# Gate sums moved into the attention stage and onto Pool, output groups on two sets of PSUM banks, last outputs issued from two queues

## The chip, the core and the metric

One core of one Trainium2 chip runs the whole kernel in one launch. The metric is device time in microseconds (us); the kernel before took 942.1 us, the median of 3 runs. TensorE (PE) does the products, VectorE (DVE) and ScalarE (ACT) work around them, GpSimd (POOL) is mostly free, and SyncE (SP) issues the transfers in the order of its queue. Each engine works through its own queue in order: an instruction that waits holds up all that stand behind it on that engine.

## What is computed

A transformer layer over 512 tokens of width 2048, in fp32. The part that matters here is the modulation: one row `mod = silu(c) @ w_ada + b_ada` is cut into shift, scale and **gate**, 2048 values each. Shift and scale are needed at the very start, gate only at the very end.

```python
mod = silu(c) @ w_ada[l] + b_ada[l]
shift, scale, gate = jnp.split(mod, 3, axis=-1)
h = rms_norm(x, norm_g[l]) * (1.0 + scale) + shift
z = h @ w_in[l]                       # u_A v_A gate_A | q k v gate_B forget_B
y_a = chunked_spatial_gating(gelu(u_a), gelu(v_a), ...) * silu(g_a)   # group A
y_b = forgetting_attention(q_b, k_b, v_b, f_b, b_f[l]) * silu(g_b)    # group B, 16 heads
y = concat([y_a, y_b]) @ w_out[l]
x = x + gate * y
return rms_norm(x, final_g)
```

## The kernel before, in words

Every weight tile is loaded as fp32 into a buffer of the ring `raw` (4 buffers, 512 KB loads), split by `w_tile` (L115) into a high part `whi` on ACT (L127) and a low part `wlo` on DVE (L128), and used in three products (hi times hi, hi times low, low times hi), so that one weight tile is 24 products of 512 columns. `whi` and `wlo` have two buffers each, so a tile is split while the tile before it is multiplied.

The stages, in the order in which PE goes through them:

- to about 240 us: shift and scale, the normalised input, the columns of u_A and part of gate_A;
- to about 620 us: branch B in four rounds u = 0 to 3 of four heads each. `g_group`, `qk_group` and `v_group` (L646 to L689) stream four weight tiles each for the gate, q, k and v columns. After each weight tile `tick()` (L131) takes one piece of attention from `slots` (scores, `lse`, probabilities, values: L472) and one piece from `fillers`. `lse` sends a row of sums back into q by eight small transfers on SP (L511), for which the second product of the probabilities waits (L528). `evac_q` clears two rows of q on POOL (L458) once that product has read the q of the round before;
- to about 710 us: the columns of v_A (`va`, L699), then `ga`, the last 256 columns of gate_A, with the mixing over chunks of branch A (`mix_head`, L727, which takes its PSUM banks by the tag `x`);
- to the end: the output projection in four groups of 512 columns (L816 to L857). Each group accumulates in four PSUM banks with the tag `mm` (`wob`, L818), one for each block of 128 tokens, and `wo_evac` (L783) multiplies a bank by the gate (L793), which also frees the bank, adds x (L799) and sums squares. The last group works from weights that were split ahead (`load_w3`, L808), block by block, and each block ends in the final norm and four output transfers from SP (L857).

PSUM has eight banks: four with the tag `mm`, and four (tags `b` and `c`) which `bank("x", ...)` (L59) gives out in turn.

**Gate** is summed in 32 steps, `gate_step(g, i)` (L594): a step loads 512 KB of `w_ada` into a buffer of the same ring `raw`, by SP, and DVE multiplies it by the values of silu(c) and adds it to `gate[:, g]`: 16 rows of 128 x 512 for each of the four groups, the first by L601 and the others by L603. `gate_sum(g)` (L605) then adds over the partitions by a product with ones (L610) and adds the bias (L611). These 36 pieces are put into `fillers` after round u = 3 (L691), and the ticks of `va`, `ga` and the output groups 0 and 1 work them off.

The order of the instructions is not the order of the code: a scheduler places each engine's instructions, so the change moves them on every queue.

Of the kernel before, what the change touches and what calls it, by code (L numbers as in the profile page):

```python
# [12 lines left out]
ALU = mybir.AluOpType  # L13
AX = mybir.AxisListType

P = 128
# [3 lines left out]
NT = S // P  # L20
# [7 lines left out]
def trunk_kernel(  # L28
# [30 lines left out]
    def bank(tag, name):  # L59
        if tag == "x":  # L60
            tag = "bbbc"[turn[0] % 4]
            turn[0] += 1
        return ps.tile([P, 512], F32, tag=tag, name=name, bufs={"mm": 4, "b": 3, "c": 1}[tag])
# [2 lines left out]
        nc.scalar.activation(hi, src, AF.Copy)  # L66
        (eng or nc.vector).tensor_tensor(lo, src, hi.bitcast(F32), ALU.subtract)

# [1 line left out]
    ident = const.tile([P, P], F32, name="ident")  # L70
    make_identity(nc, ident)
    cmask = const.tile([P, S], BF16, name="cmask")
# [17 lines left out]
        nc.vector.tensor_scalar(dst, src, mult, EPS, ALU.mult, ALU.add)  # L90
        nc.gpsimd.tensor_tensor(dst, dst, nhalf[:, 0:1], ALU.pow)

# [1 line left out]
    queue = []  # L94
    CHAIN = [1]

# [68 lines left out]
            for b in range(nb):  # L165
                evs[b](banks[b])

# [1 line left out]
    st_cm = tc.tile_pool(name="st", bufs=1)  # L169
    st = st_cm.__enter__()  # L170

# [246 lines left out]
                            evac_g(b - 8, sp[b], st)  # L418
    st_cm.__exit__(None, None, None)

# [1 line left out]
    pb_cm = tc.tile_pool(name="pb", bufs=1)  # L422
    pb = pb_cm.__enter__()
    QS = [[pb.tile([P, S], F32R, tag="qstk", bufs=8, name=f"q{i}_{j}") for j in range(2)] for i in range(4)]
# [165 lines left out]
        nc.vector.tensor_tensor_scan(f3, f1, f4, 0.0, ALU.mult, ALU.add)  # L590
        split(fsplit[:, 0, :], fsplit[:, 1, :], f3)

    # gate part of the modulation, worked off between weight tiles
    def gate_step(g, i):  # L594
        ga = wp.tile([P, 2, 512], F32, tag="raw", name=f"gate{g}_{i}", bufs=4)
        nc.sync.dma_start(ga, ada_r[:, 2 * i : 2 * i + 2, 2, g * 512 : (g + 1) * 512])
        for j in range(2):
            kk = 2 * i + j
            a = gate[:, g, :]
            if kk == 0:  # L600
                nc.vector.tensor_scalar(a, ga[:, j], sc[:, 0:1], None, ALU.mult)  # L601
            else:
                nc.vector.scalar_tensor_tensor(a, ga[:, j], sc[:, kk : kk + 1], a, ALU.mult, ALU.add)  # L603

    def gate_sum(g):  # L605
        gsl = slice(2 * D + g * 512, 2 * D + (g + 1) * 512)
# [3 lines left out]
        nc.tensor.matmul(gp, ones, gate[:, g, :], start=True, stop=True)  # L610
        nc.vector.tensor_tensor(gate[:, g, :], gp, bg, ALU.add)  # L611

    # spatial weights, worked off between weight tiles
    bias2 = gp_.tile([P, 8, P], F32, name="bias2")

    def spatial_weights():
# [49 lines left out]
    def g_group(u):  # L666
        col_group([(GB0 + u * 256, 256)], [evac_gb(2 * u), evac_gb(2 * u + 1)], f"gb{u}")
# [16 lines left out]
    for u in range(1, 4):  # L684
        if u == 1:
            fillers.append(spatial_weights)
        g_group(u)
        qk_group(u)
        v_group(u)  # L689

    for g in range(4):  # L691
        for i in range(8):
            fillers.append(lambda g=g, i=i: gate_step(g, i))
        fillers.append(lambda g=g: gate_sum(g))

# [1 line left out]
    va = [[pb.tile([P, 512], F32, tag="qstk", bufs=8, name=f"va{t}_{g}") for g in range(2)] for t in range(NT)]  # L697
    vst = [pb.tile([P, 2, 6], F32, name=f"vst{t}") for t in range(NT)]
    for g in range(2):  # L699
# [71 lines left out]
    ])  # L771
    col_group([(G0 + 768, 256)], [(lambda pt, b=b: evac_g(b, pt, pb)) for b in range(6, 8)], "ga")

# [1 line left out]
    KO = list(range(8, 16)) + list(range(8))  # L775
    for k in KO[:8]:
        split_y(k)
# [37 lines left out]

    for g in range(3):  # L816
        gsl = slice(g * 512, (g + 1) * 512)
        wob = [bank("mm", f"wo{g}_{t}") for t in range(NT)]  # L818
        for ki in range(0, KB, 2):
            k = KO[ki]  # L820
            hi, lo = w_tile([(g * 512, 512)], k, 2, src=wout_r, name=f"wo{g}_{k}")
            mm_toks(wob, 512, hi, lo, yh, yl, [k, k + 1], KO[0], KO[-1])
            tick()
        if g == 0:
            wo_evac(g, range(NT), pb, ("qstk", 8, "kstk", 8, "p", 2))
            pb_cm.__exit__(None, None, None)
            po = ctx.enter_context(tc.tile_pool(name="po", bufs=1))
            slots.extend([[] for _ in range(8)] + [[lambda i=i: load_w3(i)] for i in range(8)])
        else:
            wo_evac(g, range(NT), po, PT)  # L830
    wob = [bank("mm", f"wo3_{t}") for t in range(NT)]
    for t in range(NT):
        nc.vector.reduce_sum(sfin[:, t, 0:1], ssf[:, t, 0:3], AX.X)
        nc.vector.tensor_scalar(
            sfin[:, t, 0:1], sfin[:, t, 0:1], 1.0 / D, EPS, ALU.mult, ALU.add
        )
        tsl = slice(t * P, (t + 1) * P)
        for k in range(KB):
            hi, lo = w3[k // 2]
            j = k % 2  # L840
            nc.tensor.matmul(wob[t], yh[k][:, tsl], hi[:, j, :], start=(k == 0), stop=False)
            nc.tensor.matmul(wob[t], yl[k][:, tsl], hi[:, j, :], start=False, stop=False)
            nc.tensor.matmul(wob[t], yh[k][:, tsl], lo[:, j, :], start=False, stop=(k == KB - 1))
        wo_evac(3, [t], po, PT)
        s1 = sfin[:, t, 1:2]
        nc.vector.scalar_tensor_tensor(
            s1, ssf[:, t, 3:4], 1.0 / D, sfin[:, t, 0:1], ALU.mult, ALU.add
        )
        nc.gpsimd.tensor_tensor(s1, s1, nhalf[:, 0:1], ALU.pow)
        nc.vector.scalar_tensor_tensor(r[t][3], r[t][3], s1, fgs[3], ALU.mult, ALU.mult)  # L850
        for g in range(3):
            if g == 0:
                nc.vector.tensor_scalar(r[t][g], r[t][g], s1, None, ALU.mult)
            else:
                nc.scalar.activation(r[t][g], r[t][g], AF.Copy, scale=s1)
        for g in (1, 0, 3, 2):
            nc.sync.dma_start(out[0, t * P : (t + 1) * P, g * 512 : (g + 1) * 512], r[t][g])  # L857


_INS = ["x", "c", "norm_g", "w_ada", "b_ada", "w_in", "ln_v_g", "ln_v_b", "w_s", "b_s", "b_f", "w_out", "final_g"]  # L860
# [23 lines left out]
```

## Time and profile before

| | |
|---|---|
| device time, median of 3 runs | 942.1 us (942.01 to 943.24) |
| span of the profiled execution, first to last instruction | 944.6 us (its own device time is not given apart from the span) |
| PE busy | 902.9 us (96%) |
| DVE busy | 555.3 us (59%) |
| ACT busy | 413.0 us (44%) |
| POOL busy | 127.8 us (14%) |
| mean granted TensorE clock | 0.988 |

Where an engine is listed as busy it was executing; in brackets behind an instruction stands how long its engine was idle before it and what ended the wait. A granted clock of 1.00 is 2.4 GHz, one of 0.50 is 1.2 GHz; a value in between is a mean over a stretch that had both. A stage in which PE is busy all of the time can't be shortened by anything but fewer products; a stage in which it is not shows what it waited for.

### The profile page before, as it was taken

Reading aid. Unit: us, or ns where it says so; the run is one execution under the profiler, and the core shown is the slowest. Engines: PE = TensorE matmul, PEld = TensorE weight load, DVE = VectorE, ACT = ScalarE, POOL = GpSimd, SP = SyncE. Lnnn points to the kernel's source line nnn. Section 1 sums busy time; section 2 is a strip of 40 time slices with the busy share of each in tenths; the row PEclk is TensorE's granted clock in tenths of the full one; section 3 lists DMA queues with packets and bytes.
Section 4 is the critical chain, followed back from the end, with each engine's and each line's share of the span. In section 5 each row is a group of like instructions: output and inputs, shape, how many; then the busy total and the mean of one; then the engine's idle time right before and its main releaser. Section 6 shows DMA issues by size and latency. Waiting matters only on the chain.

```text
span 944.6 us, 12321 instructions
## 1 busy us (share of the span) xinstructions
PE 902.9 (96%) x4485; PEld 764.7 (81%) x4485; DVE 555.3 (59%) x970; ACT 413.0 (44%) x724; POOL 127.8 (14%) x110
## 2 busy tenths in 40 slices
PE   4889989999999999999999999999999998999995
PEld 4768878888888888988899888988888776878884
DVE  4777877473744455546445653757558986555522
ACT  4734423352645545665455644655315322234211
POOL 1136545514000000000000000000002220000000
PEclk9999999999999999999999999999999999999998
DMA  8999996335333232322222333344554555656222
GB/s 297 335 356 351 320 306 185 90 72 146 88 115 90 69 111 68 91 72 86 72 85 70 90 90 90 112 157 123 172 185 134 178 168 178 219 203 213 68 101 89
DMA packets 117916, 142.73 MB, mean 151 GB/s; under 512 B 8400, under 2 KB 89504, under 8 KB 117344
## 3 DMA queue, kind: packets, MB, share of 16 engines
q1 hardware_dynamic: 117856, 141.95, 47.9%
q8 instruction: 35, 0.57, 0.3%
q14 instruction: 25, 0.20, 0.1%
HBM read 137.54 MB, written 4.19 MB: 150 GB/s over the span
## 4 chain that ended last, share of the span: by engine, by line
PE 81%; DMA 5%; DVE 4%; issue 2%; ACT 1%; ACTq 0%; POOLq 0%; POOL 0%; DVEq 0%
PE s L143 5%; PE s L145 5%; PE s L144 5%; DMA gate<-in_w_ada_dram 4%; PE vb L153 3%; PE vb L154 3%; PE vb L152 3%; PE q L143 3%; PE gb L144 3%; PE gb L145 3%; PE q L145 3%; PE va L152 3%; PE va L154 3%; PE gb L143 3%; PE q L144 3%; PE va L153 3%
## 5 line engine op out<-in xcount | busy, mean ns | idle before, releaser
L143 PE MATMUL s<-hh,whi_st 128*128 128x512 f32 x224 | 87.3, 408 | 6.8 <-ACT hh L278 6.7
L144 PE MATMUL s<-hl,whi_st 128*128 128x512 f32 x224 | 87.5, 391 | 1.1 <-POOL hl L289 1.1
L152 PE MATMUL wo<-whi_wo,yh 128*128 128x512 f32 x192 | 77.2, 402 | 4.6 <-DVE r L793 4.6
L145 PE MATMUL s<-hh,wlo_st 128*128 128x512 f32 x224 | 77.4, 391 | 0.0
L603 DVE SCALAR_TENSOR_TENSOR gate<-gate,sc,gate 128x512 f32<-128x512 f32 x60 | 46.9, 782 | 50.6 <-DMA gate<-in_w_ada_dram 50.1
L153 PE MATMUL wo<-whi_wo,yl 128*128 128x512 f32 x192 | 76.2, 397 | 0.0
L253 DVE SCALAR_TENSOR_TENSOR acc<-ada,sc,acc 128x512 f32<-128x512 f32 x98 | 74.0, 755 | 3.1
L128 POOL TENSOR_TENSOR wlo_st<-raw_st,whi_st 128x1024 fp32r<-128x1024 f32 (+3 forms) x32 | 63.8, 1998 | 79.8 <-ACT whi_st L127 78.3
L154 PE MATMUL wo<-wlo_wo,yh 128*128 128x512 f32 x192 | 70.4, 399 | 3.5 <-DVE wlo_wo L128 3.5
L153 PE MATMUL vb<-whi_vb,hl 128*128 128x256 f32 (+1 forms) x256 | 71.7, 286 | 0.0
L152 PE MATMUL vb<-whi_vb,hh 128*128 128x256 f32 (+1 forms) x256 | 71.3, 284 | 0.0
L154 PE MATMUL vb<-wlo_vb,hh 128*128 128x256 f32 (+1 forms) x256 | 67.5, 285 | 0.0
L127 ACT ACTIVATE whi_st<-raw_st 128x1024 fp32r<-128x1024 f32 (+3 forms) x36 | 31.4, 873 | 78.7 <-PE s L144 29.3
L143 PEld LDWEIGHTS s<-hh,whi_st 128*128 128x128 f32 x224 | 43.4, 195 | 16.5 <-ACT hh L278 7.0
L143 PE MATMUL q<-hh,whi_q 128*128 128x512 f32 x128 | 50.5, 395 | 1.6 <-ACT ft L662 1.6
L144 PEld LDWEIGHTS s<-hl,whi_st 128*128 128x128 f32 x224 | 42.2, 188 | 10.9 <-POOL hl L289 2.3
L144 PE MATMUL gb<-hl,whi_gb 128*128 128x512 f32 x128 | 50.4, 394 | 0.0
L152 PE MATMUL va<-whi_va,hh 128*128 128x512 f32 x128 | 50.4, 395 | 0.0
L143 PE MATMUL gb<-hh,whi_gb 128*128 128x512 f32 x128 | 50.1, 391 | 0.0
L144 PE MATMUL q<-hl,whi_q 128*128 128x512 f32 x128 | 50.0, 391 | 0.0
L145 PE MATMUL gb<-hh,wlo_gb 128*128 128x512 f32 x128 | 50.0, 393 | 0.0
L153 PE MATMUL va<-whi_va,hl 128*128 128x512 f32 x128 | 50.0, 390 | 0.0
(220 smaller groups left out, 2204.5 us busy)
## 6 DMA issues: line engine op xcount, KB each, us to landing
ada<-in_w_ada_dram SPq DMA_DIRECT2D x128, 256.0 KB
gate<-in_w_ada_dram SPq DMA_DIRECT2D x32, 512.0 KB
raw_wo<-in_w_out_dram SPq DMA_DIRECT2D x24, 512.0 KB
raw_q<-in_w_in_dram SPq DMA_DIRECT2D x16, 512.0 KB
raw_k<-in_w_in_dram SPq DMA_DIRECT2D x16, 512.0 KB
raw_gb<-in_w_in_dram SPq DMA_DIRECT2D x16, 512.0 KB
raw_va<-in_w_in_dram SPq DMA_DIRECT2D x16, 512.0 KB
raw_st<-in_w_in_dram SPq DMA_DIRECT2D x21, 384.0 KB
```

Source lines behind the costliest of these rows:

```text
L127: nc.scalar.activation(hi, raw, AF.Copy)
L128: (loeng or nc.vector).tensor_tensor(lo, raw, hi.bitcast(F32), ALU.subtract)
L143: nc.tensor.matmul(pt, hi[:, j, cs], hh[k], start=(k == first), stop=False)
L144: nc.tensor.matmul(pt, hi[:, j, cs], hl[k], start=False, stop=False)
L145: nc.tensor.matmul(pt, lo[:, j, cs], hh[k], start=False, stop=(k == last))
L152: nc.tensor.matmul(o, ah[k][:, tsl], hi[:, j, :], start=(k == first), stop=False)
L153: nc.tensor.matmul(o, al[k][:, tsl], hi[:, j, :], start=False, stop=False)
L154: nc.tensor.matmul(o, ah[k][:, tsl], lo[:, j, :], start=False, stop=(k == last))
L253: nc.vector.scalar_tensor_tensor(sb if kk == KB - 1 else a, ga[:, j], sc[:, kk : kk + 1], a, ALU.mult, ALU.add,)
L603: nc.vector.scalar_tensor_tensor(a, ga[:, j], sc[:, kk : kk + 1], a, ALU.mult, ALU.add)
```

## The change

The gate's pieces are put into `fillers` at the start of round u = 1, so that the ticks of rounds 1 to 3 work them off, one between two weight tiles. Their arithmetic goes to POOL, where a product and an addition take two instructions: the loaded row is multiplied in place (L603 of the new kernel) and then added to the sum (L604). `gate_sum` itself stays on PE and DVE. The output groups 1 and 3 take their four banks by the tag `x`, groups 0 and 2 stay with `mm`. Of the last four output transfers two are issued by ACT.

```diff
@@ gate_step
             if kk == 0:
-                nc.vector.tensor_scalar(a, ga[:, j], sc[:, 0:1], None, ALU.mult)
+                nc.gpsimd.tensor_scalar(a, ga[:, j], sc[:, 0:1], None, ALU.mult)
             else:
-                nc.vector.scalar_tensor_tensor(a, ga[:, j], sc[:, kk : kk + 1], a, ALU.mult, ALU.add)
+                nc.gpsimd.tensor_scalar(ga[:, j], ga[:, j], sc[:, kk : kk + 1], None, ALU.mult)
+                nc.gpsimd.tensor_tensor(a, a, ga[:, j], ALU.add)
...
     for u in range(1, 4):
         if u == 1:
             fillers.append(spatial_weights)
+            for g in range(4):
+                for i in range(8):
+                    fillers.append(lambda g=g, i=i: gate_step(g, i))
+                fillers.append(lambda g=g: gate_sum(g))
         g_group(u)
         qk_group(u)
         v_group(u)
 
-    for g in range(4):
-        for i in range(8):
-            fillers.append(lambda g=g, i=i: gate_step(g, i))
-        fillers.append(lambda g=g: gate_sum(g))
...
-        wob = [bank("mm", f"wo{g}_{t}") for t in range(NT)]
+        wob = [bank("x" if g == 1 else "mm", f"wo{g}_{t}") for t in range(NT)]
...
-    wob = [bank("mm", f"wo3_{t}") for t in range(NT)]
+    wob = [bank("x", f"wo3_{t}") for t in range(NT)]
...
         for g in (1, 0, 3, 2):
-            nc.sync.dma_start(out[0, t * P : (t + 1) * P, g * 512 : (g + 1) * 512], r[t][g])
+            (nc.scalar if t == NT - 1 and g in (1, 2) else nc.sync).dma_start(out[0, t * P : (t + 1) * P, g * 512 : (g + 1) * 512], r[t][g])
```

How this moves the instructions is seen at three places.

SP's queue in round u = 1, from the load of the second weight tile of the gate columns (`raw_gb_4`) to the small transfers of `lse` (`lt`). Before:

```order
L121 DMA raw_gb_4_2827<-in_w_in_dram 128x4x256
L121 DMA raw_gb_8_2904<-in_w_in_dram 128x4x256
L121 DMA raw_gb_12_2982<-in_w_in_dram 128x4x256
L121 DMA raw_q_0_3035<-in_w_in_dram 128x4x256
L511 DMA q_1_1839<-lt_2630 1x4x128 x2
L511 DMA q_1_1841<-lt_2630 1x4x128 x2
```

Now, where `gate_0` to `gate_2` are the first three steps of the gate's group 0:

```order
L121 DMA raw_gb_4_2827<-in_w_in_dram 128x4x256
L596 DMA gate_0_2904<-in_w_ada_dram 128x2x512
L121 DMA raw_gb_8_2909<-in_w_in_dram 128x4x256
L596 DMA gate_1_2987<-in_w_ada_dram 128x2x512
L121 DMA raw_gb_12_2993<-in_w_in_dram 128x4x256
L596 DMA gate_2_3036<-in_w_ada_dram 128x2x512
L511 DMA q_1_1839<-lt_2630 1x4x128 x2
L511 DMA q_1_1841<-lt_2630 1x4x128 x2
```

Three loads of the gate now stand ahead of the small transfers, and the load of `raw_q_0` comes behind them instead of ahead.

POOL's queue in the same round, from the masking of the spatial weights (`ws`) on. Before:

```order
L623 AFFINE_SELECT ws<-ws 128x1024
L458 MEMSET q_1_1839 2x512
L458 MEMSET q_1_1841 2x512
```

Now:

```order
L624 AFFINE_SELECT ws<-ws 128x1024
L601 TENSOR_SCALAR gate<-gate_0_2904,sc 128x512
L603 TENSOR_SCALAR gate_0_2904<-gate_0_2904,sc 128x512
L604 TENSOR_TENSOR gate<-gate,gate_0_2904 128x512
L603 TENSOR_SCALAR gate_1_2987<-gate_1_2987,sc 128x512 x2
L604 TENSOR_TENSOR gate<-gate,gate_1_2987 128x512 x2
L603 TENSOR_SCALAR gate_2_3036<-gate_2_3036,sc 128x512 x2
L604 TENSOR_TENSOR gate<-gate,gate_2_3036 128x512
L458 MEMSET q_1_1839 2x512
L604 TENSOR_TENSOR gate<-gate,gate_2_3036 128x512
```

The clearing of q's rows now stands between two instructions of one gate step: while it waits, that step's buffer of the ring stays taken.

DVE's queue where output group 0 ends, from the low part of the last weight tile of group 0 (`wlo_wo_6`) to the evacuation of its four banks (`r_0` to `r_3` from `wo_0` to `wo_3`). Before:

```order
L128 TENSOR_TENSOR wlo_wo_6_6932<-raw_wo_6_6929,whi_wo_6_6931 128x1024
L603 SCALAR_TENSOR_TENSOR gate<-gate_1_7035,sc,gate 128x512
L611 TENSOR_TENSOR gate<-gp_6926,bg_6924 128x512
L128 TENSOR_TENSOR wlo_wo_8_7008<-raw_wo_8_7005,whi_wo_8_7007 128x1024
L603 SCALAR_TENSOR_TENSOR gate<-gate_2_7069,sc,gate 128x512
L793 TENSOR_TENSOR r_0_6965<-wo_0_6590,gate 128x512
L603 SCALAR_TENSOR_TENSOR gate<-gate_2_7069,sc,gate 128x512
L793 TENSOR_TENSOR r_1_6967<-wo_1_6591,gate 128x512
```

Now:

```order
L128 TENSOR_TENSOR wlo_wo_6_7029<-raw_wo_6_7026,whi_wo_6_7028 128x1024
L128 TENSOR_TENSOR wlo_wo_8_7101<-raw_wo_8_7098,whi_wo_8_7100 128x1024
L793 TENSOR_TENSOR r_0_7058<-wo_0_6716,gate 128x512
L799 TENSOR_TENSOR r_0_7058<-r_0_7058,xr_0_7066 128x512
L793 TENSOR_TENSOR r_1_7060<-wo_1_6717,gate 128x512
```

No piece of the gate stands in front of the first evacuation any more.

## Rows read from the trace of the kernel before

**Rows 1.** Busy time by engine in stretches of the span: stretch, its length, then for PE, PEld, DVE, ACT and POOL the busy us and the number of instructions, the granted clock, the mean busy share of the DMA engines and GB/s.

```profile
300.00:540.00 240.00, 240.00 (x1306) 208.61 (x1305) 124.34 (x257) 131.79 (x265) 5.18 (x10) 1.00 0.29 83
540.00:720.00 180.00, 180.00 (x918) 153.93 (x917) 106.58 (x191) 83.57 (x155) 2.11 (x4) 1.00 0.42 129
...
740.00:760.00 20.00, 18.97 (x92) 15.54 (x91) 18.43 (x26) 5.66 (x9) 8.62 (x5) 1.00 0.48 158
760.00:780.00 20.00, 19.26 (x98) 15.73 (x97) 17.18 (x33) 5.87 (x8) 3.62 (x2) 1.00 0.55 178
780.00:800.00 20.00, 15.52 (x65) 11.80 (x64) 10.78 (x15) 4.24 (x6) 2.13 (x1) 0.98 0.51 178
800.00:820.00 20.00, 20.00 (x84) 16.46 (x83) 14.03 (x19) 5.66 (x11) 0.00 (x0) 0.93 0.63 216
...
840.00:860.00 20.00, 18.14 (x73) 14.54 (x72) 13.82 (x19) 8.93 (x14) 0.00 (x0) 0.91 0.78 253
```

**Rows 2.** PE's waits from 720 us to the end: engine and line, what it waited for, us in total, times, the longest.

```profile
PE wo L152 <- DVE r L793: 4.6, 2, 2.8
PE wo L154 <- DVE wlo_wo L128: 3.5, 3, 1.7
```

**Rows 3.** Instructions in order of time where output group 0 hands over to group 1: start us, us, engine, line, operation.

```profile
796.45 0.75 DVE L603 SCALAR_TENSOR_TENSOR gate<-gate,sc,gate 128x512 f32<-128x512 f32 x1 [3.98 <-DMA gate<-in_w_ada_dram]
797.12 0.68 DVE L793 TENSOR_TENSOR r<-wo,gate 128x512 f32<-128x512 f32 x1
...
797.95 0.47 PE L152 MATMUL wo<-whi_wo,yh 128*128 128x512 f32 x1 [2.75 <-DVE r L793]
```

**Rows 4.** The same where group 1 hands over to group 2.

```profile
844.12 1.23 DVE L67 TENSOR_TENSOR w3l<-raw_w,w3h 128x1024 fp32r<-128x1024 f32 x1 [3.51 <-ACT w3h L66]
845.26 1.28 DVE L793 TENSOR_TENSOR r<-wo,gate 128x512 f32<-128x512 f32 x2
...
846.09 0.47 PE L152 MATMUL wo<-whi_wo,yh 128*128 128x512 f32 x1 [1.86 <-DVE r L793]
```

**Rows 5.** The four us behind each of these two hand-overs, in the columns of Rows 1.

```profile
799.00:803.00 4.00, 4.00 (x12) 3.15 (x11) 4.00 (x8) 1.63 (x5) 0.00 (x0) 0.57 0.43 131
846.00:850.00 4.00, 3.91 (x11) 3.18 (x12) 4.00 (x7) 3.17 (x6) 0.00 (x0) 0.63 0.72 249
```

**Rows 6.** The instructions that write or read the tile `gate`: durations in ns (min, median, max), first and last start; and what ended the idle time ahead of them.

```profile
L603 DVE SCALAR_TENSOR_TENSOR gate<-gate,sc,gate x60: 729/751/1789, 596.2 to 827.5; 128x512 f32<-128x512 f32 x60
...
L601 DVE TENSOR_SCALAR gate<-gate,sc x4: 485/486/486, 595.6 to 778.5; 128x512 f32<-128x512 f32 x4
...
  DMA gate<-in_w_ada_dram: 54.1, 27
```

**Rows 7.** POOL's instructions grouped by line and shape over the whole span: busy us, mean ns of one, idle time ahead of them.

```profile
L289 POOL TENSOR_TENSOR hl<-xT,hh 128x512 fp32r<-128x512 f32 x15 | 19.1, 1294 | 16.3 <-ACT xT L286 16.3
...
L67 POOL TENSOR_TENSOR vl<-va,vh 128x512 fp32r<-128x512 f32 x4 | 7.4, 1872 | 0.0
...
L429 POOL MEMSET q<- 128x512 f32 x4 | 2.1, 527 | 15.0 <-issue 15.0
...
L623 POOL TENSOR_SCALAR_AFFINE_SELECT ws<-ws 128x1024 f32<-128x1024 f32 x1 | 1.8, 1836 | 59.3 <-DMA ws<-in_w_s_dram 59.3
```

**Rows 8.** The instructions of the tiles `raw_gb` (gate columns of branch B, four weight tiles in each of the four rounds): the split on ACT, durations in ns, first and last start.

```profile
L127 ACT ACTIVATE whi_gb<-raw_gb x16: 1042/1061/1063, 269.2 to 524.9; 128x1024 fp32r<-128x1024 f32 x16
```

**Rows 9.** Instructions in order of time in the stage of v_A, where one load of the gate stands between two weight tiles.

```profile
691.53 0.37 SPq L596 DMA_DIRECT2D gate<-in_w_ada_dram  x1
...
693.73 1.06 ACT L127 ACTIVATE whi_va<-raw_va 128x1024 fp32r<-128x1024 f32 x1 [4.38 <-PE va L153]
...
695.43 1.54 DVE L603 SCALAR_TENSOR_TENSOR gate<-gate,sc,gate 128x512 f32<-128x512 f32 x2 [2.80 <-DMA gate<-in_w_ada_dram]
696.89 1.22 DVE L128 TENSOR_TENSOR wlo_va<-raw_va,whi_va 128x1024 fp32r<-128x1024 f32 x1
...
699.17 1.06 ACT L127 ACTIVATE whi_va<-raw_va 128x1024 fp32r<-128x1024 f32 x1 [4.38 <-PE va L153]
```

**Rows 10.** DVE and POOL side by side in the output projection, in order of time.

```profile
750.25 1.79 DVE L603 SCALAR_TENSOR_TENSOR gate<-gate,sc,gate 128x512 f32<-128x512 f32 x1 [1.26 <-DMA gate<-in_w_ada_dram]
751.45 5.67 POOL L67 TENSOR_TENSOR vl<-va,vh 128x512 fp32r<-128x512 f32 x3
...
754.05 1.92 DVE L128 TENSOR_TENSOR wlo_wo<-raw_wo,whi_wo 128x1024 fp32r<-128x1024 f32 x1
```

**Rows 11.** Round u = 1 in order of time: the low part of the last gate tile of round 0, the small transfers of `lse`, the product that needs them, the weight load that follows, and POOL's clearing of q.

```profile
289.49 1.22 DVE L128 TENSOR_TENSOR wlo_gb<-raw_gb,whi_gb 128x1024 fp32r<-128x1024 f32 x1
...
309.67 5.20 SPq L511 DMA_DIRECT2D q<-lt  x8
...
315.77 0.74 PE L528 MATMUL t<-q,k 128*128 128x512 f32 x4
...
316.62 0.52 POOL L458 MEMSET q<- 2x512 f32 x1 [32.54 <-PE t L528]
```

**Rows 12.** The end of the program, in order of time: the scaling of the last block and its four output transfers.

```profile
938.14 1.33 ACT L855 ACTIVATE r<-r,sfin 128x512 f32<-128x512 f32 x2 [0.85 <-POOL sfin L849]
...
938.81 0.48 DVE L853 TENSOR_SCALAR r<-r,sfin 128x512 f32<-128x512 f32 x1
938.89 1.79 SPq L857 DMA_DIRECT2D out_dram<-r  x4
```

## The prediction

> **What bounds the kernel now.** I read the busy time by stretches first. In the attention stage and in the stage of v_A PE is busy without a gap, 240.00 of 240 us and 180.00 of 180 us, at a granted clock of 1.00, while POOL is busy 5.18 of 240 us and DVE about half [rows 1]. Nothing can be won there, only lost. In the output projection PE has gaps: 1.03, 0.74, 4.48 and 1.86 us in the four stretches that begin at 740, 760, 780 and 840 us, 8.1 us together [rows 1]. PE's waits name the same 8.1 us: 4.6 us for DVE's evacuation of an output bank (L793) and 3.5 us for DVE's low parts of weights (L128) [rows 2]. So DVE, in order, is what PE waits for.
>
> Why DVE is late shows where the groups hand over. At 796.45 DVE has waited 3.98 us for a load of the gate, and the evacuation stands behind it in the queue; PE waits 2.75 us [rows 3]. At 844.12 it has waited 3.51 us for the high part of a weight of the last group, the evacuation again behind it; PE waits 1.86 us [rows 4]. Both waits exist because the next group takes the four banks that the last one has just filled. The gate holds DVE for 60 instructions of 782 ns and 4 of 486 ns, 48.9 us, and makes it wait 54.1 us for loads [rows 6].
>
> A wait costs twice here. In the four us behind each hand-over the granted clock is 0.57 and 0.63 [rows 5], a mixture of the two levels 2.4 and 1.2 GHz, after PE had stood idle 2.75 and 1.86 us. From the stretches this is 0.02, 0.07 and 0.09 of 20 us, 3.6 us [rows 1]. The gaps of about 1 us, in the stretches that begin at 740 and 760, left the clock at 1.00 [rows 1].
>
> **The change, part by part.** *Removed from DVE:* 48.9 us of gate sums and the 54.1 us of waits for loads, all between 595 and 828 us [rows 6]. Of this only what delays L793 and L128 lies on the path: the wait of 2.75 us [rows 3] goes wholly, and of the 3.5 us for low parts [rows 2] I keep 0.7, since the mixing of branch A and POOL's work beside it still load DVE at 740 to 780 us. What is late next there is DVE's mixing.
>
> *Banks.* Group 1 no longer needs the banks of group 0, nor group 2 those of group 1: DVE has a whole group's time to empty them, so the 1.86 us of [rows 4] go even though the queue in front of L793 still holds a split that waits for its load. The last mixing, early in group 0, has to have left the x banks; DVE, freed of the gate, gets there sooner. With both long waits gone the 3.6 us of clock go too.
>
> *Moved to POOL:* 64 products and 60 additions of 128 x 512. An addition is 1.294 us when POOL is undisturbed and 1.872 us beside a busy DVE [rows 7]; DVE is half busy in the stage, so I take 1.5. A product has one tensor to read and no row of its own. It lies between 0.53 (a memset of this size, which reads nothing) and 1.87 us (the disturbed two-input form) [rows 7]; half of the 1024-element masking, 0.92 us, is the nearest row and my value. One step of two rows is then 2 x (0.92 + 1.5) = 4.8 us, between 3.6 and 7.5. The Trainium skill (GPSIMD Engine Reference, section 3.1) has 769 ns for a tight one-input loop of 512 elements; by that a step would be an estimated 4.5 us.
>
> Against this stands the pace of the weight tiles. From the first to the last split of the `gb` tiles lie 39 tiles in 255.7 us, 6.56 us each [rows 8]; the bare tile is 5.44 us (from 693.73 to 699.17) [rows 9]. POOL keeps pace at 4.8 us, in a stretch where it was almost idle: its time costs nothing.
>
> *Ring and SP's queue.* Every step takes one of the four `raw` buffers, now for the load (3.9 us from its issue to DVE's start [rows 9]) plus 4.8 us, in place of 3.9 + 1.54. With two buffers for the gate that is 8.7 us in every 10.9 to 13.1 us. The stage of v_A, which alternated gate and weights in the same ring, had no gap on PE [rows 1]. In round 1 the spatial weights sit in one of the four buffers too, so it is tightest there.
>
> The sharp spot is `lt` in round 1: the third gate load now stands ahead of the eight small transfers. The first gate load can go when the low part at 289.49 is done, at 290.7 [rows 11]. I read the next two as each waiting for POOL to release the one before: 290.7 + 3.9 + 4.8 = 299.4, then 308.1, just ahead of the 309.67 at which the small transfers go [rows 11]. They take 0.65 us each to issue, so the first pair is out by 311.0 and the product that needs it starts at 315.77 [rows 11]: 4.8 us of slack, of which 3.9 us of gate data ahead may take most. I charge nothing for it, but 1.5 us in all for this and similar spots in three rounds.
>
> *The clearing of q* on POOL waits for that same product; it waited 32.54 us [rows 11]. Behind it now stand gate steps, whose buffers SP needs. Since SP, PE and POOL go round together this only moves the slack above. *The four products of `gate_sum`* move with the steps; they are as long as before, and PE would wait for POOL there if POOL were late.
>
> *DVE in the attention stage* shares with POOL: beside POOL's subtractions a gate instruction took 1.79 us instead of 0.75, and a low part 1.92 instead of 1.22 [rows 6, 9, 10]. A low part that comes 0.7 us later still comes about 2 us before its tile, since it is made 2.3 us after its buffer comes free and the tile before lasts 5.44 us [rows 9]. The Trainium skill says (SBUF — State Buffer, section Who interferes with whom) that a DVE instruction with two SBUF inputs contends with a GpSimd instruction that reads SBUF, the later one blocking fully. By full blocking a low part could come up to one POOL instruction late and rival 3 would be likelier. The rows show 0.7 to 1.0 us of delay, less than that.
>
> *Outputs.* The last four transfers are issued from 938.89 in 1.79 us, 0.45 each [rows 12]. ACT ends its scaling at 939.47 and could issue its second at 939.9, SP's fourth started at about 940.2: 0.3 us, bounds 0 to 0.4.
>
> **The sum.** 8.1 + 3.6 + 0.3 = 12.0 us at best; less 0.7 for low parts and 1.5 in the attention stage is 9.8 us. The profiled execution spans 944.6 us, 2.5 above the median 942.1 and above all three runs, so I use differences only: 942.1 − 9.8 = **932.3 us**, and 930.1 if nothing is lost.
>
> **The rivals.**
> 1. *The attention stage gives part back.* With steps of 6.3 us the chain above reaches the third gate load at 311.1 in place of 308.1, and the small transfers are some 2 us late at the product: three rounds of 1.0 to 2.7 us with the clock behind them (1.7 us, as at 799 [rows 5]) are 3 to 8 us, about 937 us. For it: two loads that stood behind POOL. Against: 4.8 us of slack. Chance 0.16.
> 2. *The wait moves within the output projection.* The evacuation no longer matters, but low parts and weight loads stay late (3.5 us of waits [rows 2], and the load wait of [rows 4] is not the gate's). Half of the gain: 936 us. Chance 0.09.
> 3. *Slower: POOL sets the pace of the attention stage.* If all four instructions of a step take the disturbed 1.87 us [rows 7], a step is 7.5 us, above the 6.56 us of a tile; the ring then holds weights back, and 32 steps cost 32 x (7.5 − 6.56) = 30 us: 962. It decides from a step of 6.56 + 9.8/32 = 6.9 us on; a step of 7.1 us gives 950 us, at which I price it. For it: contention is in the trace. Against: POOL's undisturbed row is 1.294, and DVE is free half of the time. Chance 0.12.
> 4. *The change doesn't do what it says:* whatever follows the gate in DVE's queue waits for loads just as long, and PE's gaps only move. Against: no load but the gate's holds DVE at 796 [rows 3]. 941 to 943 us, chance 0.06.
>
> **How the numbers follow.** My forecast, 930 to 936 us, has 0.57. Two runs are told apart from 0.2% on, some 2 us. Faster by more than that holds the forecast and rivals 1 and 2, 0.82, less 0.02 for the upper end of rival 1: 0.80. Within 0.2%: rival 4 and that end, 0.08. Slower: 0.12. The range goes from the best case, 930.1, less 1 us for what the sum can't place, up through rivals 1 and 2 to 942, and leaves out rival 3 and part of rival 4.
>
> **What would show it.** Right: PE's waits for L793 gone, at most about 1 us for L128 after 720 us, the granted clock at 1.00 from 740 to 860 us, PE still full from 300 to 540 us, and POOL near 150 us busier (64 x 0.92 + 60 x 1.5). Wrong: PE waiting at L528, at `gp` or for low parts in rounds 1 to 3; weight loads on SP waiting for POOL by several us; a POOL step above 6.5 us.

## The result and the profile after

The changed kernel takes **935.06 us** (median of 4 runs, 934.63 to 936.01), the kernel before 942.17 us (4 runs beside them, 942.01 to 943.24). The ratio is 0.9916, with a 95% interval of 0.9899 to 0.9933. The forecast was 932.3 us in a range of 929 to 942. The profiled execution of the change took 936.01 us, its span is 934.3 us.

The stretches of [rows 1] in the kernel after, in the same columns:

```profile
300.00:540.00 240.00, 239.30 (x1294) 206.83 (x1293) 147.83 (x261) 130.01 (x265) 204.18 (x132) 1.00 0.49 151
540.00:720.00 180.00, 180.00 (x923) 154.39 (x922) 84.56 (x153) 82.32 (x155) 2.32 (x4) 1.00 0.31 91
...
740.00:760.00 20.00, 20.00 (x107) 17.10 (x105) 17.87 (x27) 9.34 (x14) 9.31 (x6) 1.00 0.17 54
760.00:780.00 20.00, 20.00 (x98) 16.89 (x97) 13.72 (x25) 5.72 (x7) 2.59 (x2) 1.00 0.46 158
780.00:800.00 20.00, 20.00 (x90) 16.53 (x90) 11.31 (x16) 5.91 (x12) 0.00 (x0) 1.00 0.31 95
...
840.00:860.00 20.00, 20.00 (x90) 16.57 (x89) 12.80 (x16) 9.03 (x15) 0.00 (x0) 1.00 0.67 222
```

PE is now full through the output projection, at a granted clock of 1.00. POOL went from 5.18 to 204.18 us in the attention stage and DVE there from 124.34 to 147.83, though all that came to it there were three bias additions of `gate_sum`, 2.1 us: its instructions beside POOL became longer. The one wait of PE between 290 us and the last product, where [rows 2] had two lines:

```profile
PE k L143 <- DVE q L455: 0.7, 1, 0.7
```

At the place of [rows 3], where output group 0 ends, DVE evacuates without a load ahead of it, in order of time:

```profile
795.80 0.68 DVE L793 TENSOR_TENSOR r<-wo,gate 128x512 f32<-128x512 f32 x1
796.40 1.21 DVE L128 TENSOR_TENSOR wlo_wo<-raw_wo,whi_wo 128x1024 fp32r<-128x1024 f32 x1
```

The gate's rows, which were DVE's in [rows 6], by line and shape (busy us, mean ns of one, idle time ahead):

```profile
L603 POOL TENSOR_SCALAR gate<-gate,sc 128x512 f32<-128x512 f32 x60 | 108.6, 1818 | 21.5 <-DMA gate<-in_w_ada_dram 20.0 <-DVE tm L552 1.3 <-DVE nm L490 0.2
L604 POOL TENSOR_TENSOR gate<-gate,gate 128x512 f32<-128x512 f32 x60 | 88.2, 1470 | 2.4
...
L601 POOL TENSOR_SCALAR gate<-gate,sc 128x512 f32<-128x512 f32 x4 | 7.1, 1775 | 21.7 <-DMA gate<-in_w_ada_dram 21.7
```

The three rows sum to 203.9 us, 6.37 us for each of the 32 steps; a full step of two products and two additions is 2 x (1.818 + 1.470) = 6.58 us. SP now waits for it (queue and line, us in total, times, longest):

```profile
SPq L121 <- POOL gate L604: 52.5, 18, 5.9
SPq L596 <- POOL gate L604: 52.2, 13, 8.6
```

The gb tiles of [rows 8], and the end of the program, which was [rows 12]:

```profile
L127 ACT ACTIVATE whi_gb<-raw_gb x16: 1042/1060/1065, 272.3 to 532.3; 128x1024 fp32r<-128x1024 f32 x16
```

```profile
928.39 1.33 ACT L855 ACTIVATE r<-r,sfin 128x512 f32<-128x512 f32 x2 [0.85 <-POOL sfin L849]
...
929.14 0.95 ACTq L857 DMA_DIRECT2D out_dram<-r  x2
929.17 0.81 SPq L857 DMA_DIRECT2D out_dram<-r  x2
```

The gb tiles now take 260.0 us instead of 255.7; three products of `gate_sum` and the wait of 0.7 us stand in that stretch. The most useful reading of all the traces is one table. Four marks are taken from each trace, which is one execution: the first split of gb (start of round 0's last part), the first product of v_A (`va<-whi_va`), the first of the output projection (`wo<-whi_wo`), the last product (`wo<-w3l`); the fifth is the span's end. The differences, in us:

| kernel | median us | ratio to before (95%) | gb at | to v_A | to output | to last product | to end |
|---|---|---|---|---|---|---|---|
| before, profile shown ahead | 942.17 | | 269.2 | 348.0 | 121.5 | 195.9 | 10.0 |
| before, once more (e1) | 942.85 | 1.0007 (0.9990, 1.0024) | 273.7 | 348.1 | 122.3 | 188.6 | 10.0 |
| banks only (e2) | 943.52 | 1.0009 (0.9994, 1.0024) | 272.3 | 348.1 | 122.1 | 189.8 | 10.0 |
| gate only (e3) | 935.81 | 0.9927 (0.9905, 0.9949) | 269.3 | 352.5 | 121.8 | 180.5 | 9.5 |
| outputs only (e4) | 943.26 | 1.0005 (0.9988, 1.0021) | 270.6 | 348.0 | 122.1 | 188.2 | 9.8 |
| **the change** | **935.06** | **0.9916 (0.9899, 0.9933)** | 272.3 | **352.2** | 121.8 | **178.6** | 9.4 |
| gate early on DVE (e5) | 951.31 | 1.0096 (1.0066, 1.0126) | 271.1 | 367.3 | 121.8 | 178.6 | 9.7 |
| gate late on POOL (e6) | 966.26 | 1.0253 (1.0220, 1.0287) | 272.1 | 348.1 | 130.5 | 208.6 | 9.6 |
| products on ACT (e7) | 952.93 | 1.0108 (1.0080, 1.0135) | 272.3 | 370.2 | 121.8 | 178.6 | 9.4 |
| 32 products more (e8) | 982.64 | 1.0425 (1.0397, 1.0454) | 272.0 | 399.2 | 121.8 | 178.6 | 9.4 |
| quicker products (e9) | 945.47 | 1.0021 (1.0004, 1.0038) | 270.7 | 364.2 | 121.8 | 178.6 | 9.4 |
| 16 products more (e10) | 949.56 | 1.0061 (1.0044, 1.0078) | 271.5 | 368.2 | 121.8 | 178.6 | 9.7 |
| outputs on one queue (e11) | 934.63 | 0.9908 (0.9890, 0.9926) | 270.6 | 352.1 | 121.9 | 178.5 | 9.6 |
| quicker products, lt pinned (e12) | 937.83 | 0.9949 (0.9926, 0.9972) | 270.9 | 355.6 | 121.8 | 178.7 | 9.4 |

The change takes 9.6 to 17.3 us out of the output projection and puts 4.2 us into the attention stage. Much of the 4.2 is not a loss: the four products of `gate_sum`, 1.02 us each in the trace, moved there (before they stood at 672, 739, 787 and 838 us). Nor is all of the 9.6 to 17.3 us a gain: three of those products left the output projection, and twelve products of the mixing, some 1.4 us, now stand ahead of its mark (40 behind it instead of 52).

### The profile page after: what moved, and what is told of

Its sections match the earlier page's. It is cut to its first block, busy times and chain, and to the rows that moved or that the text cites. A ratio compares the mean times of both kernels' runs of the same rounds, so it can differ in the third digit from the quotient of the medians.

```text
span 934.3 us, 12387 instructions
## 1 busy us (share of the span) xinstructions
PE 899.5 (96%) x4485; PEld 764.7 (82%) x4485; DVE 537.0 (57%) x906; ACT 412.0 (44%) x724; POOL 325.5 (35%) x234
## 4 chain that ended last, share of the span: by engine, by line
PE 86%; issue 2%; DMA 1%; DVE 1%; ACT 1%; POOL 1%; SPq 0%; POOLq 0%; ACTq 0%; DVEq 0%
PE s L143 5%; PE s L145 5%; PE s L144 5%; PE wo L154 5%; PE wo L153 5%; PE wo L152 5%; PE vb L153 3%; PE vb L154 3%; PE vb L152 3%; PE va L153 3%; PE k L143 3%; PE va L154 3%; PE va L152 3%; PE k L144 3%; PE k L145 3%; PE gb L144 3%
## 5 line engine op out<-in xcount | busy, mean ns | idle before, releaser
L603 POOL TENSOR_SCALAR gate<-gate,sc 128x512 f32<-128x512 f32 x60 | 108.6, 1818 | 21.5 <-DMA gate<-in_w_ada_dram 20.0
L128 POOL TENSOR_TENSOR wlo_st<-raw_st,whi_st 128x1024 fp32r<-128x1024 f32 (+3 forms) x32 | 63.8, 1999 | 82.8 <-ACT whi_st L127 81.3
L604 POOL TENSOR_TENSOR gate<-gate,gate 128x512 f32<-128x512 f32 x60 | 88.2, 1470 | 2.4
L152 PE MATMUL wo<-whi_wo,yh 128*128 128x512 f32 x192 | 74.8, 390 | 0.0
L91 POOL TENSOR_TENSOR rsv<-rsv,nhalf 128x1 f32<-128x1 f32 x4 | 4.6, 1149 | 165.4 <-DVE rsv L90 165.4
L849 POOL TENSOR_TENSOR sfin<-sfin,nhalf 128x1 f32<-128x1 f32 x4 | 2.2, 548 | 152.3 <-DVE sfin L846 152.3
L143 PE MATMUL k<-hh,whi_k 128*128 128x512 f32 x128 | 50.4, 394 | 0.7 <-DVE q L455 0.7
```

What stands on the lines that cost most here:

```text
L128: (loeng or nc.vector).tensor_tensor(lo, raw, hi.bitcast(F32), ALU.subtract)
L143: nc.tensor.matmul(pt, hi[:, j, cs], hh[k], start=(k == first), stop=False)
L152: nc.tensor.matmul(o, ah[k][:, tsl], hi[:, j, :], start=(k == first), stop=False)
L603: nc.gpsimd.tensor_scalar(ga[:, j], ga[:, j], sc[:, kk : kk + 1], None, ALU.mult)
L604: nc.gpsimd.tensor_tensor(a, a, ga[:, j], ALU.add)
```

## The experiments

**The kernel before, once more.** No edit.

> The kernel before, unchanged, to see how far its executions differ. The profiled execution of before spans 944.6 us, but the changed kernel's four runs took 1.7 us more than their spans, so a typical run of before (942.2 us) should span about 940.5. Theory A (the profile fell on a costly execution): spans of 940 to 941 us, and a profile whose stops in the output projection or whose first 240 us differ from the first profile by 3 to 4 us. Theory B (the ACT queue adds time outside the span in the changed kernel): spans near 944 us with device times 2 us below them.

Measured: 942.85 us, and a profiled execution of 944.38 us whose output projection is 7.3 us shorter than in the profile the forecast used. Its waits of PE from 720 us on, and a stretch behind the stop at the first hand-over (2.57 us, until 800.16):

```profile
PE wo L152 <- DVE r L793: 3.5, 2, 2.6
PE wo L154 <- DVE wlo_wo L128: 0.9, 1, 0.9
PE mix L739 <- DVE mt L748: 0.3, 1, 0.3
```

```profile
800.00:804.00 4.00, 3.84 (x17) 3.20 (x18) 4.00 (x8) 1.45 (x4) 0.00 (x0) 1.00 0.46 156
```

The waits are 4.7 us instead of 8.1, and the clock stayed at 1.00 behind a stop almost as long as the one that gave 0.57 in [rows 5]. So what the output projection loses differs from execution to execution of the same program, and so does the first mark (269.2 against 273.7).

**Banks alone**, the gate left where it was:

```
-        wob = [bank("mm", f"wo{g}_{t}") for t in range(NT)]
+        wob = [bank("x" if g == 1 else "mm", f"wo{g}_{t}") for t in range(NT)]
...
-    wob = [bank("mm", f"wo3_{t}") for t in range(NT)]
+    wob = [bank("x", f"wo3_{t}") for t in range(NT)]
```

> Only the two sets of banks; the gate stays late and on DVE. Theory A (a hand-over costs because the next group needs the banks that DVE has yet to empty): PE's waits for L793 and the slow clock behind them go (4.6 + 3.6 us of the profile of before), the waits for low parts (3.5 us) stay: ratio 0.991 to 0.995, some 934 to 938 us. Rival (DVE held up by the gate is the cause by itself, and PE would then wait for the low parts of the next group, which stand behind the same gate instruction): ratio 0.997 to 1.000, the wait of 2.75 us reappearing at L154.

Measured: 943.52 us, no gain. PE's waits from 720 us on:

```profile
PE wo L154 <- DVE wlo_wo L128: 2.7, 3, 1.3
PE wo L152 <- ACT whi_wo L127: 1.9, 3, 1.4
```

The wait for L793 is gone, as the banks promise, and 4.6 us of others stand there. DVE still stood 3.49 us for a gate load at 796.50, and what is late behind it then is a weight's low part, whose buffer SP needs for the next load. The banks took away the wait that was named, and not what caused it.

**The gate alone**, early and on POOL (the diff's parts at L598 to L604 and L684 to L691):

> Only the gate: early and on POOL; all output groups on the same four banks, outputs from SP. Theory A: the wait of 2.75 us behind group 0, the waits for low parts and the clock behind the first hand-over go; the wait of 1.9 us behind group 1, where a split waits for its own load, and the clock behind it stay if the split still stands ahead of the evacuation: ratio 0.992 to 0.996. If the gate is the whole cause, the ratio is that of the full change, 0.9925 or less.

Measured: 935.81 us; the one wait of PE for L793 left from 720 us on is 0.2 us. Against the change its ratio (0.9927 against 0.9916) leaves nothing that could be told apart from zero for banks and outputs together, though its output projection is 1.9 us longer in the profiles.

**Outputs alone** (the diff's part at L857):

> Only the last outputs from two queues. Theory A: the profile's end is 0.3 to 0.6 us nearer to the last product and the device time falls by as much, ratio 0.9994 to 0.9997. Theory B (a second queue costs time outside the span): device time minus span grows by 1 to 2 us and the ratio is 1.000 to 1.002.

Measured: 943.26 us, no gain. The device time stands 1.7 us above the span here, in the change and in the other profiled executions, so nothing is hidden outside the span. The **change without this part** tells the same:

> As the change, with all final transfers on SP's queue again. The forecast's term: 0.3 us slower than the change (0 to 0.4), 935.4 us. If the two queues matter more than the issue time, 936 us or more; if they don't help at all, 935 us. By the profile: the last transfer issued about 0.3 us later after the last product, and the tail behind the last product 9.7 us instead of 9.4.

Measured: 934.63 us (934.27 to 938.26), the same as the change. The four issues on one queue are

```profile
927.40 1.80 SPq L857 DMA_DIRECT2D out_dram<-r  x4
```

and the tail behind the last product is 9.6 us instead of 9.4. With two queues the tails of the other kernels go from 9.4 to 9.8 us, with one from 9.5 to 10.0, so the term isn't told apart from zero, neither in the time nor in the profiles.

**The place without the engine.** The change, but its steps run on DVE (the first product of each group, not shown, as well):

```
-                nc.gpsimd.tensor_scalar(ga[:, j], ga[:, j], sc[:, kk : kk + 1], None, ALU.mult)
-                nc.gpsimd.tensor_tensor(a, a, ga[:, j], ALU.add)
+                nc.vector.scalar_tensor_tensor(a, ga[:, j], sc[:, kk : kk + 1], a, ALU.mult, ALU.add)
```

> The gate's steps stand early, as in the change, but run on DVE with the one-instruction form of before; banks and outputs as in the change. Place theory (what counts is that no gate step and no gate load stands in the output projection, whichever engine sums): DVE has room in the attention stage (124 of 240 us busy, and 48.9 us come on), so 934 to 936 us, no wait of PE for L793 or L128 after 720 us, a gate step of about 1.54 us. Engine theory (the gate has to leave DVE's queue as well, since 32 waits of up to 4 us for gate loads stand ahead of low parts of weights and of evacuations): PE waits for DVE in the attention stage, 5 us or more in all, and 939 to 943 us, or slower than before.

Measured: 951.31 us, slower than before. The output projection is as good as the change's (178.6 us); the attention stage loses 15.1 us more. What ended the waits of the gate's instructions, and PE's longest waits from 290 to 600 us:

```profile
  DMA gate<-in_w_ada_dram: 62.5, 31
```

```profile
PE k L143 <- DVE q L455: 2.3, 1, 2.3
PE q L145 <- DVE wlo_q L128: 1.8, 1, 1.8
PE k L145 <- DVE wlo_k L128: 1.6, 1, 1.6
PE vb L154 <- DVE wlo_vb L128: 0.9, 1, 0.9
```

DVE did not run out of time (154.55 of 240 us busy from 300 to 540); it stood 62.5 us for gate loads, in order, with low parts and q's differences behind. The place theory fell.

**The engine without the place.** The change, but the 36 fillers are appended behind the third round, as before.

> The gate's sums run on POOL but stand where they stood before, behind the third round; banks and outputs as in the change. Engine theory (DVE's queue is what counted): PE's waits for L793 and L128 are gone and the time is 935 to 937 us. Place theory: the gate's loads and the ring buffers that POOL now holds for 6.6 us a step stand in the stages whose tiles last 5.44 us, so weight loads come late there, PE waits for high and low parts in v_A or the output projection, and the time is 940 us or more; if POOL sets the pace for all 32 steps there it could be 32 x 1.1 = 35 us slower than the change.

Measured: 966.26 us, 24 us slower than before. PE from 720 us on:

```profile
PE wo L152 <- ACT whi_wo L127: 16.2, 8, 5.0
PE ga L145 <- DVE wlo_ga L128: 1.8, 2, 1.1
```

PE no longer waits for L793; it waits for weights, whose ring buffers POOL holds where a tile lasts 5.44 us [rows 9]: from 690 to 900 us SP's weight loads waited 28.2 us for the sums on POOL. So neither half of the gate's edit gains anything by itself: late on DVE 942, early on DVE 951, late on POOL 966, early on POOL 935.

**Less work for POOL.** The 64 products run on ACT as scaled copies (the first of each group, not shown, as well), the additions stay on POOL:

```
-                nc.gpsimd.tensor_scalar(ga[:, j], ga[:, j], sc[:, kk : kk + 1], None, ALU.mult)
+                nc.scalar.activation(ga[:, j], ga[:, j], AF.Copy, scale=sc[:, kk : kk + 1])
```

> As the change, but the 64 products run on ACT as scaled copies (about 0.6 us each, 38 us in all, by ACT's rows of 128x512) and only the 60 additions stay on POOL, so that POOL is busy some 110 us less. If POOL's 6.58 us a step are wholly hidden: 935 us, no change against the change. If its slowness costs PE something in the attention stage (the ring, or DVE's contention with it): 933 to 934 us, and DVE's low parts nearer to 1.3 us than to 1.69. If ACT's order suffers (copies that wait for gate loads ahead of exponentials and high parts): PE waits for ACT in the attention stage, 938 us or more.

Measured: 952.93 us. ACT stood 57.8 us for gate loads ahead of its products, and PE waited where it had not:

```profile
PE o L543 <- ACT pth L66: 4.1, 2, 3.6
PE o L543 <- DVE ptl L67: 2.5, 3, 1.3
```

By these rows it is the same as on DVE: a load wait put into the queue of an engine that PE waits for.

**More work for POOL.** One product by 1.0 more in each step, then in every second step (`if j and i % 2:`):

```
+                if j:
+                    nc.gpsimd.tensor_scalar(ga[:, j], ga[:, j], 1.0, None, ALU.mult)
                 nc.gpsimd.tensor_tensor(a, a, ga[:, j], ALU.add)
```

> As the change, with one more product by 1.0 on POOL in each step (32 in all, the result is the same), so that a step takes 6.6 + 1.8 = 8.4 us, or 7.9 to 8.4 if the form without a scalar's pointer is quicker. Pace theory, as in the forecast's third rival (a step above about 6.9 us costs PE the difference): 32 x (8.2 - 6.9) = 42 us slower than the change, about 977 us. Rival: the steps are spread over a longer stretch than the gb tiles (the gate's sums end at 364 and 562 us in the change, 8.2 us a step), so a step of up to 8.2 us is hidden: 935 to 938 us.

> As the kernel with one more product on POOL in each step, but in every second step alone: 16 products of 1.5 to 1.9 us, a mean step of some 7.3 us. No slack (the change's step of 6.58 us stands just at the pace, every us more costs PE one): 16 x 1.5 = 24 us, 959 us. Slack (a long step is made up for by the next short one, and the threshold of 6.9 us of the forecast's third rival holds for the mean): 32 x (7.3 - 6.9) = 13 us or less, 935 to 948 us.

Measured: 982.64 and 949.56 us, 47.6 and 14.5 us above the change. POOL's gate rows with 32 products more:

```profile
L603 POOL TENSOR_SCALAR gate<-gate,sc 128x512 f32<-128x512 f32 x60 | 98.2, 1646 | 44.6 <-DMA gate<-in_w_ada_dram 41.0 <-DVE nm L490 2.2 <-DVE q L455 1.0
L606 POOL TENSOR_TENSOR gate<-gate,gate 128x512 f32<-128x512 f32 x60 | 87.4, 1457 | 1.4
L605 POOL TENSOR_SCALAR gate<-gate 128x512 f32<-128x512 f32 x32 | 54.9, 1717 | 0.4
L601 POOL TENSOR_SCALAR gate<-gate,sc 128x512 f32<-128x512 f32 x4 | 6.6, 1659 | 14.6 <-DMA gate<-in_w_ada_dram 14.6
```

They sum to 247.1 us, 7.72 us a step; with 16 more it is 6.99 us; in the change 6.37 us. Against the pace of 6.56 us from [rows 8] that is 32 x 1.16 = 37 us and 32 x 0.43 = 14 us too long, and 0 for the change. The second agrees with 14.5, the first is 10 us short of 47.6. PE's longest waits with 32 more are for weights:

```profile
PE k L143 <- ACT whi_k L127: 9.9, 4, 4.7
```

A threshold at the pace itself, a few tenths of a us above the change's step, fits the second size and not the first, and it is not shown. (The 6.9 us in the expectations was the forecast's break-even against the kernel before; against the change the loss would have to begin at 6.56. With 16 products more the time lies above the range given with slack, 935 to 948 us, and below the 959 us without.) POOL was not full in either kernel: its gate rows are busy for 84% of the time from the first to the last in the change and for 81% with 32 products more. SP, which waited 52.5 and 52.2 us for POOL in the change, waited less with them:

```profile
SPq L121 <- POOL gate L606: 22.2, 14, 3.4
SPq L596 <- POOL gate L606: 10.7, 4, 3.9
```

And the order on SP's queue is another in both; what that alone can cost, the next kernel shows.

**The same work in a quicker form.** In 60 of the 64 products the scalar's column is read as a second input, broadcast along the row:

```
-                nc.gpsimd.tensor_scalar(ga[:, j], ga[:, j], sc[:, kk : kk + 1], None, ALU.mult)
+                nc.gpsimd.tensor_tensor(ga[:, j], ga[:, j], sc[:, kk : kk + 1].to_broadcast([P, 512]), ALU.mult)
```

> As the change, but 60 of POOL's 64 products are written as two-input multiplications with the scalar column broadcast along the row. Form theory (the product with a scalar pointer is a slow form by itself: median 1.565 us undisturbed against 1.29 for the addition): a product takes 1.3 us, a step 5.2 to 5.9 us instead of 6.58. Read theory (POOL's time goes by what it reads and writes, or a broadcast operand is no cheaper): 1.5 us or more, no change of the step. In either case PE is already full in the attention stage, so the time is 934 to 936 us; only if the change still pays for POOL there (rival 1 of the forecast) it is 932 to 934 us.

Measured: the product is quicker, median 1041 ns instead of 1565, and the kernel is **10.4 us slower than the change**, 945.47 us. None of the expectations had that. The product and the place:

```profile
L603 POOL TENSOR_TENSOR gate<-gate,sc x60: 1031/1041/2029, 297.6 to 541.9; 128x512 f32<-128x512 f32 x60
```

```profile
415.56 0.37 SPq L121 DMA_DIRECT2D raw_gb<-in_w_in_dram  x1
421.15 0.34 SPq L609 DMA_DIRECT2D bg<-in_b_ada_dram  x1
421.59 0.39 SPq L121 DMA_DIRECT2D raw_gb<-in_w_in_dram  x1
422.02 5.05 SPq L511 DMA_DIRECT2D q<-lt  x8
...
426.37 1.41 PE L528 MATMUL t<-q,k 128*128 128x512 f32 x4 [5.32 <-DMA q<-lt]
```

In the change the same queue has the small transfers ahead of the bias and the weights:

```profile
410.74 0.37 SPq L121 DMA_DIRECT2D raw_gb<-in_w_in_dram  x1
413.90 5.10 SPq L511 DMA_DIRECT2D q<-lt  x8
419.10 0.39 SPq L609 DMA_DIRECT2D bg<-in_b_ada_dram  x1
419.58 0.38 SPq L121 DMA_DIRECT2D raw_gb<-in_w_in_dram  x1
```

The program's order on SP is laid down when it is built; the other form of the product moved ten of SP's entries, and in round 2 the small transfers came to stand behind two loads that wait for ring buffers. PE stood 5.32 us and then ran at half clock until about 432.5 (a granted clock of 0.83 from 420 to 440 us). To test this, the last kernel **pins the order** and leaves the quicker product:

```
+            if g == 1:
+                es.enter_context(tc.issue_after(last_lt[0].ins))
             nc.sync.dma_start(bg, b_ada[:, gsl].broadcast_to([P, 512]))
...
+                    if last_lt[0] is not None and name in ("gb2_12", "gb3_12"):
+                        es.enter_context(tc.issue_after(last_lt[0].ins))
```

> As the kernel whose products are two-input multiplications, but the eight small transfers of lt in rounds 2 and 3 are pinned ahead of the gate's bias load and of the last gb weight load, where the change has them; the quicker POOL step (4.7 us) stays. Queue theory (that kernel lost its 10 us against the change because its order on SP puts the small transfers behind two loads that wait for ring buffers, so that PE waited 5.3 us at L528 and ran at half clock for 4 us behind it): the 5.3 and the 0.7 us of waits and some 2.3 us of slow clock come back, and with what hangs on them the time is 935 to 938 us. Rival (a quicker POOL step is itself what hurts, because it lets gate loads go earlier and crowd the weights): PE waits elsewhere in the attention stage and the time stays at 942 to 946 us. If the quicker step were worth something: under 934 us.

Measured: 937.83 us, 7.6 less. The small transfers go at 416.24 and PE's waits for `lt` are gone; what is left from 290 to 600 us is

```profile
PE k L147 <- DVE q L459: 1.9, 1, 1.9
PE gp L618 <- POOL gate L608: 0.4, 1, 0.4
```

The order of SP's queue was the cause of some seven tenths of the loss. The attention stage is still 3.4 us longer than the change's, which is what the rows add up to: 1.9 us instead of 0.7, 0.4 at `gp`, and a clock of 0.91 from 360 to 380 us (1.8 us). The quicker step itself gained nothing; PE was full already in the change, 239.30 of 240 us. In e5, e7, e8 and e10 the order on SP and PE differs from the change's as well; how much of their loss is order was not taken apart, so that there the waits named are what is shown.

## Why the prediction was right, and where it was off

**What bounds the kernel: right.** DVE's queue in the output projection, with gate loads in front of L793 and L128. The gate alone gives the gain (935.81), and with any gate that is gone from there by 600 us the output projection lasts 178.5 to 180.5 us.

**The size of that gain: too large.** The terms 8.1 us of waits and 3.6 us of slow clock came from one execution that spans 944.6, and the forecast, though it noted that this is 2.5 us above the median and above all runs, subtracted them from the median. In the second execution the waits are 4.7 us and the clock term is 0; with outputs alone they are 2.9 us and 0.09 of 20 us. The output projection lost 195.9 − 178.6 = 17.3 us against the first execution and 10.0 against the second, and of that three of the four 1.02-us products and 1.4 us of mixing only moved. The sum of 9.8 us was 7.1 by the medians. With the second execution's terms the same sum would have been 4.7 + 0 + 0.3 − 0.7 − 1.5 = 2.8 us: 7.1 lies between the two, and that the forecast came as near as it did is in part luck.

**Banks: wrong as a term of its own.** The forecast booked the 1.86 us of [rows 4] to them. Alone they bring nothing (e2); with the gate gone, L793 is on time without them to 0.2 us (e3). They may be worth the 1.9 us between 180.5 and 178.6 in the profiles, but the times don't tell that from zero.

**Outputs: not told apart from zero**, where 0.3 us was said, with bounds of 0 to 0.4.

**POOL's step: mis-sized, and the cover was thinner than said.** The product was put at 0.92 us and is 1.818 us on the mean, 1.565 by the median; the addition was put at 1.5 and is 1.470. The step is 6.58 instead of 4.8 us, and POOL is busier by 197.7 instead of 150 us. The forecast itself named a step above 6.5 us as a sign that it was wrong, and weight loads on SP that wait for POOL by several us as another; both came (5.9 us at the longest), and PE was full all the same. That it was is luck as far as the forecast goes: with 0.62 us more a step, and the order that came with it, e10 is slower than the kernel before, which is the outcome of rival 3. From which step on POOL costs PE time stays open. Of the Trainium skill's 769 ns (GPSIMD Engine Reference, section 3.1) no run shows anything near: the quickest product of this size here is 1031 ns, in the two-input form.

**The loss in the attention stage: right in size (1.5 us said).** 4.2 us more, for which four products of at most 1.02 us and one wait of 0.7 us account; only the wait is a loss. The chain at `lt` that the forecast called sharp (rival 1) ran some 2 us later than it worked out: the third gate load went at 313.78 instead of 308.1, the small transfers at 314.24 instead of 309.67, of which 3.1 us are that execution's later start (gb at 272.3 instead of 269.2); and PE did not wait. That the mechanism of rival 1 exists is shown by e9, in another round: there it is the order on the queue, not POOL's pace, that decides.

**DVE beside POOL: milder than said on the mean, worse at the most, and covered.** The low parts from 300 to 540 us in the kernel after, by tile:

```profile
L128 DVE TENSOR_TENSOR wlo_gb<-raw_gb,whi_gb 128x1024 fp32r<-128x1024 f32 x12 | 15.3, 1276 | 14.4 <-ACT whi_gb L127 14.3
L128 DVE TENSOR_TENSOR wlo_k<-raw_k,whi_k 128x1024 fp32r<-128x1024 f32 x8 | 13.5, 1690 | 7.3 <-ACT whi_k L127 7.3
L128 DVE TENSOR_TENSOR wlo_vb<-raw_vb,whi_vb 128x1024 fp32r<-128x1024 f32 x8 | 13.1, 1643 | 9.6 <-ACT whi_vb L127 9.5
L128 DVE TENSOR_TENSOR wlo_q<-raw_q,whi_q 128x1024 fp32r<-128x1024 f32 x8 | 9.8, 1226 | 8.6 <-ACT whi_q L127 8.5
```

Over these tiles the mean is 1.44 us against 1.22 us undisturbed [rows 9], less than the 0.7 us more that the forecast took, but the longest low part was 2.30 us, 1.08 more. Which of the two engines starts first decides who is late:

```profile
375.22 3.51 POOL L604 TENSOR_TENSOR gate<-gate,gate 128x512 f32<-128x512 f32 x2
375.31 2.28 DVE L128 TENSOR_TENSOR wlo_k<-raw_k,whi_k 128x1024 fp32r<-128x1024 f32 x1 [1.49 <-ACT whi_k L127]
```

The eight low parts that started with 0.56 us or more of an addition on POOL still to run took 1.64 to 2.30 us, those behind a product on POOL at most 1.59; where the low part was first, POOL's instruction became longer, as the product beside the low part at 332.81, 3.01 us. The Trainium skill (SBUF — State Buffer, section Who interferes with whom) has the ports that DVE and GpSimd share as an exclusive lock, with the order of issue deciding who blocks; the trace agrees for the additions, with up to 1.08 us of delay. PE waited for no low part there: the 2 us by which they were early covered it.

## What to carry to other kernels

When a wait for a load holds an engine that others wait for, move it to an engine whose queue holds nothing urgent *and* to a stage with room for the slower step; here each of the two moves by itself made the kernel slower. Size such a gain from the spread of several executions, and not from one profile's waits and clock. Look at the order of the DMA queue after every edit, a quickening one too: small transfers that came to stand behind two loads cost 7.6 us here.

## What the runs showed of the hardware beyond that

- A product of 128x512 by a scalar column on POOL took 1565 ns (median), by a constant 1490 ns (e8), and as a two-input multiplication with the column broadcast 1041 ns (e9); the addition of two full tiles took 1292 ns. The one-input form was the slowest.
- The output projection took 195.9 and 188.6 us in two executions of the same program. The times of the kernels with the gate late on DVE spread on one chip from 938.95 to 946.75 us (65 runs), those of the change from 934.63 to 936.01 (4 runs), and with its outputs on one queue from 934.27 to 938.26 (6 runs).
- Stops of 2.75 and 2.57 us at the same place were followed by a clock of 0.57 in one execution and of 1.00 in another, and the shorter stop of 1.86 us by one of 0.63 [rows 4, 5]: how long PE stood does not decide it alone.
